# Cutting the last tile of a split-GELU kernel into steps of 1, 1, 2 and 4 rows

## Chip, cores, metric

One core of a Trainium2 chip. The metric is device time in microseconds (us), as a median of several executions; small is good. The profile's span is about 1.8 us shorter than the time of the same run, because it counts from the first to the last instruction.

## The reference

```python
x = randn(32, 512, 2048)                 # float32
x1, x2 = x[..., :1024], x[..., 1024:]
out = 0.5 * x1 * (1 + erf(x1 / sqrt(2))) * x2    # float32, (32, 512, 1024)
```

134 MB are read and 67 MB written, with one GELU and one product per output element.

## The kernel before

The 16,384 rows are cut into 16 tiles of 128 partitions x 8 rows. A tile is loaded by one transfer (8.39 MB) from SyncE's queue, two tiles ahead. ScalarE and VectorE work on it in two steps of four rows. The output of tiles 0 to 13 is stored by ScalarE's queue, 4.19 MB each; that of tile 14 by SyncE's queue; and the last tile has two stores of four rows (2.10 MB each) on SyncE's queue, each issued as soon as its four rows are done.

```python
    R, STEP = 8, 4
    ...
    xpool = ctx.enter_context(tc.tile_pool(name="xpool", bufs=2))
    opool = ctx.enter_context(tc.tile_pool(name="opool", bufs=2))
    ...
    for i in range(n_tiles):
        x_tile = ahead.pop(0)
        o_tile = opool.tile([P, R, half], out.dtype, name="o_tile")
        last = i == n_tiles - 1
        for r in range(0, R, STEP):
            rows = slice(r, r + STEP)
            nc.scalar.activation(                      # GELU, in place
                out=x_tile[:, rows, :half], in_=x_tile[:, rows, :half], func=GELU
            )
            nc.vector.tensor_mul(                      # product
                out=o_tile[:, rows, :], in0=x_tile[:, rows, :half], in1=x_tile[:, rows, half:],
            )
            if last:
                store(nc.sync, i, o_tile, rows)
        if not last:
            store(nc.sync if i == n_tiles - 2 else nc.scalar, i, o_tile, slice(0, R))
        if i + 2 < n_tiles:
            ahead.append(load(i + 2))
```

Of the kernel before, what the change touches and what calls it, by code (L numbers as in the profile page):

```python
# [1 line left out]

# [4 lines left out]

GELU = mybir.ActivationFunctionType.Gelu


@with_exitstack
def kernel(
    ctx: ExitStack,
    tc: tile.TileContext,
    x: bass.AP,
    out: bass.AP,
):





    nc = tc.nc
    P = nc.NUM_PARTITIONS

    x_flat = x.flatten_outer_dims()
    out_flat = out.flatten_outer_dims()
    n_rows, dim = x_flat.shape
    half = dim // 2

    R, STEP = 8, 4
    x_t = x_flat.rearrange("(n p r) d -> n p r d", p=P, r=R)
    o_t = out_flat.rearrange("(n p r) d -> n p r d", p=P, r=R)
    n_tiles = x_t.shape[0]

    xpool = ctx.enter_context(tc.tile_pool(name="xpool", bufs=2))
    opool = ctx.enter_context(tc.tile_pool(name="opool", bufs=2))

    def load(i):
        x_tile = xpool.tile([P, R, dim], x.dtype, name="x_tile")  # L40
        nc.sync.dma_start(out=x_tile, in_=x_t[i])  # L41
        return x_tile

    def store(queue, i, o_tile, rows):
        queue.dma_start(out=o_t[i][:, rows, :], in_=o_tile[:, rows, :])

    ahead = [load(0), load(1)]
    for i in range(n_tiles):
        x_tile = ahead.pop(0)
        o_tile = opool.tile([P, R, half], out.dtype, name="o_tile")  # L50
        last = i == n_tiles - 1
        for r in range(0, R, STEP):
            rows = slice(r, r + STEP)
            nc.scalar.activation(  # L54
                out=x_tile[:, rows, :half], in_=x_tile[:, rows, :half], func=GELU
            )
            nc.vector.tensor_mul(  # L57
                out=o_tile[:, rows, :],
                in0=x_tile[:, rows, :half],
                in1=x_tile[:, rows, half:],  # L60
            )
            if last:
                store(nc.sync, i, o_tile, rows)
        if not last:
            store(nc.sync if i == n_tiles - 2 else nc.scalar, i, o_tile, slice(0, R))
        if i + 2 < n_tiles:
            ahead.append(load(i + 2))


# [1 line left out]
_INS = ['x']  # L71
_OUTS = [((32, 512, 1024), 'float32')]


# [23 lines left out]
```

## Time and profile before

| | before |
|---|---|
| time, median of the first three runs | 471.6 us |
| span of the profiled run | 469.7 us |
| last load lands | 449.29 us |
| last product ends | 461.78 us |
| last store lands | 468.9 us |

Engine columns give the busy time, its share of the span and the number of instructions. The row of DMA digits is the busy share of the 16 DMA engines in 40 equal slices, in tenths. A timeline line has the start, the duration, the engine and line of the kernel, the operation, output and input, and in brackets how long the engine sat idle before it and what ended that. "SPq" and "ACTq" are the sequencers of SyncE and ScalarE, and such a line shows only the issue of a transfer; the transfer itself is told by its time "to landing". The prediction shows the lines of the kernel before.

One warning about the chain of waits of this kernel. It ends with the last tile's GELU and product, as if they set the end, because it follows instructions and no instruction but the closing wait stands behind the last store. That wait is in SyncE's own view of waits (waited for: us in total, times, longest us):

```profile
SPq L93 <- DMA out_dram<-o_tile: 6.6, 1, 6.6
```

### The profile page before, as it was taken

The page shows a single profiled execution, that of the slowest core. Times are in us where ns is not written, and L with a number is a line of the kernel's source. Part 1 is how long each engine was busy: PE and PEld are TensorE (multiplying, and loading weights), DVE is VectorE, ACT ScalarE, POOL GpSimd, SP SyncE. Part 2 cuts the span into 40 slices and gives each one's busy share as a digit, 9 for nine tenths or more (in the row PEclk, how much of TensorE's full clock was granted, in tenths as well). Part 3 has the DMA queues.
Part 4 walks back from the last instruction along what each step waited for, and adds up shares of the span by engine and source line. Part 5 has one row for each costly group of instructions (what it writes and reads, how often), then busy time and mean ns, then how long its engine had stood idle before and what let it go on. Part 6 is the DMA issues. An engine that isn't in the chain of part 4 may idle for free.

```text
span 469.7 us, 213 instructions
## 1 busy us (share of the span) xinstructions
DVE 140.2 (30%) x32; ACT 115.2 (25%) x33; POOL 0.2 (0%) x4
## 2 busy tenths in 40 slices
DVE  0070704307042070520606115060250702507043
ACT  1052306023060320603206041060500505005060
POOL 0000000000000000000000000000000000000000
DMA  8999999999999999999999999999999999999988
GB/s 357 446 446 357 446 446 446 402 446 458 391 446 444 433 463 402 435 413 491 402 419 430 491 402 402 446 491 402 402 446 480 413 402 444 449 446 402 474 375 357
DMA packets 4754, 201.35 MB, mean 429 GB/s; under 512 B 528, under 2 KB 528, under 8 KB 528
## 3 DMA queue, kind: packets, MB, share of 16 engines
q1 hardware_dynamic: 2736, 142.61, 70.5%
q10 hardware_dynamic: 2016, 58.72, 29.0%
q14 instruction: 2, 0.02, 0.0%
HBM read 134.22 MB, written 67.11 MB: 429 GB/s over the span
## 4 chain that ended last, share of the span: by engine, by line
DMA 77%; DVE 14%; ACT 6%; DVEq 1%; issue 0%; SPq 0%; ACTq 0%
DMA x_tile<-in_x_dram 77%; DVE o_tile L57 14%; ACT x_tile L54 6%; DVEq L93 1%; SPq L41 0%; ACTq L54 0%
## 5 line engine op out<-in xcount | busy, mean ns | idle before, releaser
L57 DVE TENSOR_TENSOR o_tile<-x_tile 128x4096 f32<-128x4096 f32 x32 | 140.2, 4422 | 321.6 <-ACT x_tile L54 321.6
L54 ACT ACTIVATE x_tile<-x_tile 128x4096 f32<-128x4096 f32 x32 | 114.0, 3608 | 340.5 <-DMA x_tile<-in_x_dram 340.5
L54 ACT ACT_TABLE_LOAD x1 | 1.3, 1283 | 0.7 <-PEq L82 0.7
L82 POOL MEMSET const-bfloat16-1.0<- 128x1 bf16 x1 | 0.1, 102 | 0.0
L82 POOL MEMSET const-uint8-127<- 128x1 uint8 x1 | 0.1, 101 | 0.0
L82 POOL MEMSET const-float32-0.0<- 128x1 f32 x1 | 0.1, 99 | 0.2 <-issue 0.2
L82 POOL MEMSET const-float32-1.0<- 128x1 f32 x1 | 0.1, 98 | 0.0
## 6 DMA issues: line engine op xcount, KB each, us to landing
out_dram<-o_tile ACTq DMA_DIRECT2D x14, 4096.0 KB, 41.8
out_dram<-o_tile SPq DMA_DIRECT2D x1, 4096.0 KB, 24.8
out_dram<-o_tile SPq DMA_DIRECT2D x2, 2048.0 KB, 6.9
x_tile<-in_x_dram SPq DMA_DIRECT2D x16, 45.5
```

Source lines behind the costliest of these rows:

```text
L54: nc.scalar.activation(out=x_tile[:, rows, :half], in_=x_tile[:, rows, :half], func=GELU)
L57: nc.vector.tensor_mul(out=o_tile[:, rows, :], in0=x_tile[:, rows, :half], in1=x_tile[:, rows, half:],)
L82: nc = _bacc.Bacc("TRN2", target_bir_lowering=False, num_devices=1)
L93: with _tile.TileContext(nc) as tc:
```

## The change

The intent: the first product of the last tile has to wait for a GELU of four rows, 3.6 us. With a first step of one row it waits for 1.05 us, so VectorE starts sooner, and both stores of the last tile can be issued sooner. The stores keep their size and their queue.

```diff
-    R, STEP = 8, 4
+    R = 8
@@
-        for r in range(0, R, STEP):
-            rows = slice(r, r + STEP)
+        for lo, hi in ((0, 1), (1, 2), (2, 4), (4, 8)) if last else ((0, 4), (4, 8)):
+            rows = slice(lo, hi)
@@
-            if last:
-                store(nc.sync, i, o_tile, rows)
+            if last and hi % 4 == 0:
+                store(nc.sync, i, o_tile, slice(hi - 4, hi))
```

## The prediction

> **What bounds the kernel now.** I read the page from the top: busy shares, the row of 40 slices, the DMA queues, then the chain that ended last. The whole kernel moves 201 MB and computes little.
>
> ```profile
> span 469.7 us, 213 instructions
> DVE 140.2 (30%) x32; ACT 115.2 (25%) x33; POOL 0.2 (0%) x4
> DMA  8999999999999999999999999999999999999988
> q1 hardware_dynamic: 2736, 142.61, 70.5%
> q10 hardware_dynamic: 2016, 58.72, 29.0%
> HBM read 134.22 MB, written 67.11 MB: 429 GB/s over the span
> ```
>
> VectorE and ScalarE are busy 30% and 25% of the time; the 16 DMA engines are at 8 or 9 tenths in every slice, and the two queues together take 99.5% of their time. So the transfers set the time, and computing faster can help only in a stretch in which the DMA engines would otherwise have nothing to do. The change touches only the last tile, so the question is whether there is such a stretch after the last load has landed.
>
> The queue sizes say who shares a queue. One load is 128 x 8 x 2048 x 4 bytes = 8.39 MB, one whole store is 4.19 MB, a half store 2.10 MB. 16 x 8.39 + 4.19 + 2 x 2.10 = 142.6 MB: this is q1, the queue of SyncE, with all loads and the last three stores. 14 x 4.19 = 58.7 MB is q10, ScalarE's queue, with the other 14 stores. Next the timeline of the end (start us, duration us, engine, line, operation):
>
> ```profile
> 405.29 0.36 ACTq L45 DMA_DIRECT2D out_dram<-o_tile  x1
> 434.51 27.63 SPq L45 DMA_DIRECT2D out_dram<-o_tile  x3
> 449.37 7.12 ACT L54 ACTIVATE x_tile<-x_tile 128x4096 f32<-128x4096 f32 x2 [20.18 <-DMA x_tile<-in_x_dram]
> 453.02 8.76 DVE L57 TENSOR_TENSOR o_tile<-x_tile 128x4096 f32<-128x4096 f32 x2 [18.54 <-ACT x_tile L54]
> ```
>
> The last load lands at 449.29 (the chain of waits has its DMA piece from 405.29 for 44.00 us) and ScalarE starts at 449.37. The last store from ScalarE's queue was issued at 405.29; a store there takes 41.8 us in the middle of the queue view's list, so it lands at about 447.1. After 449.3 the transfers are SyncE's three stores alone. Asked in narrow windows, the view of the output tensor gives each of these its issue and landing time:
>
> ```profile
> 434.51 0.35 SPq L45 DMA_DIRECT2D out_dram<-o_tile  x1
> DMA to landing us min/median/max: 24.8/24.8/24.8
> ...
> 457.48 0.34 SPq L45 DMA_DIRECT2D out_dram<-o_tile  x1
> DMA to landing us min/median/max: 6.6/6.6/6.6
> ...
> 461.81 0.33 SPq L45 DMA_DIRECT2D out_dram<-o_tile  x1
> DMA to landing us min/median/max: 7.1/7.1/7.1
> ```
>
> So the store of tile 14 lands at 434.51 + 24.8 = 459.3, the first half of the last tile at 457.48 + 6.6 = 464.1, the second half at 461.81 + 7.1 = 468.9; the program ends at 469.7, 0.8 us later. The steps between landings, from the last load on, are 10.0, 4.8 and 4.8 us for 4.19, 2.10 and 2.10 MB: 419, 437 and 437 GB/s. The middle of the kernel repeats two loads and two stores, 25.17 MB, every 57.9 us (the chain's DMA pieces start at 56.85, 114.92, 172.94): 434 GB/s. The two half stores thus follow each other at the full rate of the kernel. The store of tile 14, issued 15 us before the last load landed, stood behind that load in the same queue and fills the time in which the last tile is computed. Wider stretches agree:
>
> ```profile
> 449.29:459.31 10.02, 6.29 (x2) 7.12 (x2) 0.00 (x0) 1.00 0.97 418
> 459.31:468.40 9.09, 2.47 (x1) 0.00 (x0) 0.00 (x0) 1.00 0.96 406
> ```
>
> The last two columns are the DMA share and GB/s: 0.97 and 0.96 up to the end. Single microseconds swing between 0.5 and 1.5, because whole packets are put to one window, so a gap of a few tenths can't be excluded from the shares alone; the landing times are the better witness.
>
> **What the Trainium skill says.** "DMA: Bandwidth & Descriptors", section "Queues, rings and completion order": on each DMA engine the descriptors of one queue are consumed in ring order. The trace agrees: tile 14's store, 24.8 us under way, lands 10.0 us after the load ahead of it. Same page, "Where 436 GB/s comes from": the ports give 435.2 GB/s. The trace shows 434 in the steady part and 437 between the last landings (4.8 us rounded to a tenth), so there is no faster rate to be had in the tail. Same page, "Anatomy of one DMA": its fit, made on the GpSimd path, is 2.0 us plus bytes over 436 GB/s, which for 2.10 MB is 6.8 us. The trace has 6.6 and 7.1, which is close, and this feeds the main rival below. "VectorE: DVE Perf Modes", section "The TRN2 errata": ScalarE takes 224 cycles at 1.2 GHz besides one cycle per element, and an f32 tensor_tensor (N+151)/0.96 ns. For 4096 elements this is 3600 and 4424 ns; the trace has 3608 and 4422.
>
> **The change part by part.** Removed: one GELU and one product of 4096 elements per partition. Added: GELUs and products of 1024, 1024 and 2048. Both stores stay, with their bytes, queue and order. No other tile changes, so everything up to 449.37 stays.
>
> Estimated durations from those formulas, which the trace confirms for the one size it has: GELU 1.05 us for 1024, 1.90 for 2048, 3.61 for 4096 (as measured); product 1.22, 2.29, 4.42. Instructions on one engine overlap a little: the second GELU started at 452.90, 3.53 us after the first (0.08 less than its duration), and two products took 8.76, a step of 4.34 (also 0.08 less). I take 0.08 off each step, and 0.04 from a GELU's end to the product it releases.
>
> GELU ends: 450.42, 451.39, 453.21, 456.74; before, 456.49 (two more instructions at about 0.12 each). Products: the first 450.46 to 451.68; the second 451.60 to 452.82; the third waits for its GELU, 453.25 to 455.54; the fourth waits too, 456.78 to 461.20. Stores are issued about 0.04 after the product: the first half at 455.58 instead of 457.48, 1.90 us earlier; the second at 461.24 instead of 461.81, 0.57 us earlier. The second gains so little because ScalarE must still do all eight rows before the last product can start.
>
> Now the queue. Tile 14's store still lands at 459.3, since the load before it lands when it did. The first half is in the queue 3.7 us before that instead of 1.8, and lands at 459.3 + 4.8 = 464.1 as before. The second half is issued 2.9 us before that instead of 2.3, and lands at 468.9 as before. All 1.90 and all 0.57 us turn into longer time in the queue. Sum: 0.0 us on the path that sets the end, so 471.6 us, less a tenth for what the landings, rounded to a tenth, may hide: 471.5.
>
> **The rivals.** First: the end hangs on the issue of the second half, a fixed cost plus its wire time, rather than on the queue. For it: 7.1 us is near the 6.8 of the fit. Against it: the first half lands in 6.6 though tile 14's store still has 1.8 us to go at its issue, and 1.8 + 4.8 is exactly 6.6, as 2.3 + 4.8 is 7.1. If it is true, the end moves with the issue, at most 0.57 us: 471.0.
>
> Second: the queue ran dry for a moment before the first half, as start-up and tile 14's last bytes did not quite overlap; the weak microsecond 457 to 458, share 0.53, could be that. Against it: other microseconds are as weak (447 to 448 has 0.00, with a load in flight), and the step to the next landing is the plain wire time. The most it can give: 8.39 MB at 435.2 GB/s is 19.3 us, the trace has 19.6 from the last load's landing to the last store's. So at best 0.3 us: 471.3.
>
> Third: the steps cost more than estimated, or another wait appears. To lengthen the kernel, the second half's issue would have to come some 2 us later; two small GELUs with 0.12 us extra each are far from that. It would give 472 or a little more. I hold it for unlikely.
>
> **Range and chances.** The causes reach from 471.0 to 471.6. The three runs of the kernel before spread from 471.57 to 472.48, and a median of new runs can fall anywhere there or a few tenths below. So 471.5, with 470.8 to 472.2 for 8 in 10. A gain of 2% would be 9.4 us, more than the whole 7.9 us from the last product's end to the end of the span, and nothing in the change can save that; a loss of 2% would need a different state of the chip. Faster 0.01, same 0.98, slower 0.01.
>
> **What would show it.** In the changed kernel: four GELUs and four products after the last load, the first store issued near 455.6 and the second near 461.2 on the same clock. If I am right, their times to landing grow by the same amounts, to about 8.5 and 7.7 us, and the landings stay 4.8 us apart after tile 14's. If landing times stay at 6.6 or 7.1 and the span shrinks by half a microsecond, the first rival holds; if only the step to the first half's landing shrinks, the second. A change before 449 us, or a last product that ends later than 461.8, would make the working wrong.

## The result, and the profile after

The changed kernel takes 471.43 us (median of six runs, 471.36 to 471.85), the kernel before 471.54 us (six runs, 471.3 to 472.48). The ratio is 0.9997, with a 95% interval of 0.9984 to 1.001: no difference.

The page of the changed kernel:

```profile
span 470.1 us, 217 instructions
DVE 140.5 (30%) x34; ACT 115.4 (25%) x35; POOL 0.2 (0%) x4
DMA  8999999999999999999999999999999999999988
q1 hardware_dynamic: 2736, 142.61, 70.5%
```

The same queues with the same packets, the same DMA row, and two more instructions on each of the two engines. The profiled run was the slowest of the six (471.85 us, span 470.1); the other five have spans of 469.6 and 469.7. Its last load landed at 449.81, 0.52 us later than in the profile before, although nothing is changed up to there. So I count from the last load's landing in each profile.

The end of the timeline, and the two half stores of the last tile in the view of the output tensor, asked in narrow windows:

```profile
449.89 7.31 ACT L55 ACTIVATE x_tile<-x_tile 128x1024 f32<-128x1024 f32 x4 [20.42 <-DMA x_tile<-in_x_dram]
450.98 2.36 DVE L58 TENSOR_TENSOR o_tile<-x_tile 128x1024 f32<-128x1024 f32 x2 [16.23 <-ACT x_tile L55]
453.73 2.29 DVE L58 TENSOR_TENSOR o_tile<-x_tile 128x2048 f32<-128x2048 f32 x1 [0.39 <-ACT x_tile L55]
457.23 4.43 DVE L58 TENSOR_TENSOR o_tile<-x_tile 128x4096 f32<-128x4096 f32 x1 [1.21 <-ACT x_tile L55]
...
456.05 0.34 SPq L46 DMA_DIRECT2D out_dram<-o_tile  x1
DMA to landing us min/median/max: 8.4/8.4/8.4
...
461.69 0.33 SPq L46 DMA_DIRECT2D out_dram<-o_tile  x1
DMA to landing us min/median/max: 7.6/7.6/7.6
```

VectorE starts 1.17 us after the load instead of 3.73, but then waits twice for ScalarE (0.39 and 1.21 us), because ScalarE must do all eight rows in any case. From the last load's landing:

| us after the last load has landed | before | after |
|---|---|---|
| tile 14's store lands | 10.0 | 9.8 |
| first half issued / lands | 8.19 / 14.8 | 6.24 / 14.6 |
| second half issued / lands | 12.52 / 19.6 | 11.88 / 19.5 |

The issues come 1.95 and 0.64 us sooner; the times to landing grow from 6.6 to 8.4 and from 7.1 to 7.6; and the landings stay where they were, within the 0.2 us by which tile 14's store also differs. SyncE now waits that much longer at the end:

```profile
SPq L94 <- DMA out_dram<-o_tile: 7.1, 1, 7.1
```

It was 6.6. The time won on the engines has become waiting for the queue.

### The profile page after: what moved, and what is told of

Same layout as the page of the kernel before. It is cut to its first block, busy times and chain, and to the rows that moved or that the text cites. A ratio compares the mean times of both kernels' runs of the same rounds, so it can differ in the third digit from the quotient of the medians. Undisturbed runs are those within 1.5% of the kernel's fastest.

```text
span 470.1 us, 217 instructions
## 1 busy us (share of the span) xinstructions
DVE 140.5 (30%) x34; ACT 115.4 (25%) x35; POOL 0.2 (0%) x4
## 4 chain that ended last, share of the span: by engine, by line
DMA 77%; DVE 14%; ACT 7%; issue 0%; ACTq 0%; SPq 0%
DMA x_tile<-in_x_dram 77%; DVE o_tile L58 14%; ACT x_tile L55 7%; ACTq L94 0%; SPq L42 0%; ACTq L55 0%
## 5 line engine op out<-in xcount | busy, mean ns | idle before, releaser
L58 DVE TENSOR_TENSOR o_tile<-x_tile 128x4096 f32<-128x4096 f32 (+2 forms) x34 | 140.5, 4171 | 321.2 <-ACT x_tile L55 321.2
L55 ACT ACTIVATE x_tile<-x_tile 128x4096 f32<-128x4096 f32 (+2 forms) x34 | 114.2, 3407 | 341.0 <-DMA x_tile<-in_x_dram 341.0
```

Source lines behind the costliest of these rows:

```text
L55: nc.scalar.activation(out=x_tile[:, rows, :half], in_=x_tile[:, rows, :half], func=GELU)
L58: nc.vector.tensor_mul(out=o_tile[:, rows, :], in0=x_tile[:, rows, :half], in1=x_tile[:, rows, half:],)
```

## The experiments

**Theory**: the last three stores stand in one queue behind each other, and wire time sets the end. (Wire time is a transfer's bytes over the steady rate: 4.8 us for a half store, by the step between the last two landings.) **Rival**: the end hangs on when the second half is issued, and the 0.6 us that the issue gained was lost in noise or given back elsewhere. The runs were made in three calls, each on one chip. In the four runs of the first call the kernel before had a median of 471.57 us, in the next three 471.52, in the last two 471.57.

### The stores without the wait for the last tile

```diff
-                store(nc.sync, i, o_tile, slice(hi - 4, hi))
+                store(nc.sync, i, prev, slice(hi - 4, hi))     # prev: tile 14's output
@@
+        prev = o_tile
```

This gives a wrong result: the two half stores read the output tile of tile 14, so that they wait for nothing of the last tile, which is still computed.

> The changed kernel, but the two last stores read the output tile before it (wrong result on purpose), so they are issued right behind the store of tile 14, about 14 us before the last load lands; the last tile is still computed. Queue theory: the three stores land 19.3 to 19.6 us after the last load as before, the time moves by less than 0.3 us: nothing that computes the last tile sooner can gain more than this. Issue rival: with both issues 20 us earlier the span falls to where compute or wire ends, several us less.

Measured: 471.39 us (five runs, 471.34 to 471.79), ratio to before 0.9999 (0.9987 to 1.0012). The last load landed at 449.21. The store of tile 14 and the two half stores:

```profile
434.05 0.35 SPq L46 DMA_DIRECT2D out_dram<-o_tile  x1
DMA to landing us min/median/max: 25.1/25.1/25.1
...
434.44 0.47 SPq L46 DMA_DIRECT2D out_dram<-o_tile  x1
DMA to landing us min/median/max: 29.5/29.5/29.5
...
434.97 0.42 SPq L46 DMA_DIRECT2D out_dram<-o_tile  x1
DMA to landing us min/median/max: 33.9/33.9/33.9
```

The second half was in the queue 27 us sooner than in the changed kernel, and landed at 434.97 + 33.9 = 468.9, or 19.7 us after the load. That is no sooner than before (19.6). So nothing that computes the last tile faster can shorten this kernel, and the rival falls.

### Making the second half late

```diff
+            if last and hi == R:
+                for _ in range(k):                     # k = 1, 2, 6
+                    nc.vector.tensor_mul(out=o_tile[:, 7:8, :], in0=x_tile[:, 7:8, :half],
+                                         in1=x_tile[:, 7:8, half:])
             if last and hi % 4 == 0:
```

The last row's product is done again, which changes no value and costs about 1.25 us each time (some 1.1 had been expected).

> The changed kernel, with the product of the last row of the last tile done once more before the second half store: its issue comes about 1.14 us later, some 13.0 us after the last load has landed instead of 11.9; the result is unchanged. Queue theory (the stores stand in one queue and the wire sets the end): span and time move by 0 to 0.3 us, the second half's time to landing shrinks from 7.6 to about 6.5. Rival, the end hangs on the issue of the second half: time to landing stays 7.6 and the span grows by 1.1 us.

> The same with two repeated rows: issue about 2.2 us later, some 14.1 us after the last load. Queue theory with no start-up cost: still 0. Queue theory with a fixed cost of about 2 us that needs the store to be issued that long before its turn: the second half lands at about 14.1 + 6.8 = 20.9 us after the load instead of 19.5, the span grows by about 1.5 us. Issue rival: plus 2.2 us.

> The same with six repeated rows: issue about 6.8 us later, some 18.7 us after the last load, when the first half has long landed (14.6). This measures the time to landing of a half store in an empty queue: 4.8 us if it is wire time alone (span plus 4.0), 6.8 us with a fixed cost of 2 us (span plus 6.0). Issue rival: 7.6 us and span plus 6.8.

The second half store in the three profiles, k = 1, 2, 6 in this order:

```profile
462.17 0.33 SPq L46 DMA_DIRECT2D out_dram<-o_tile  x1
DMA to landing us min/median/max: 6.7/6.7/6.7
```

```profile
463.74 0.33 SPq L46 DMA_DIRECT2D out_dram<-o_tile  x1
DMA to landing us min/median/max: 6.3/6.3/6.3
```

```profile
468.68 0.33 SPq L46 DMA_DIRECT2D out_dram<-o_tile  x1
DMA to landing us min/median/max: 6.3/6.3/6.3
```

| k | last load lands | second half issued after it | to landing | time, median (range) | against before |
|---|---|---|---|---|---|
| 1 | 449.03 | 13.14 | 6.7 | 471.53 (471.41 to 471.74) | 1.0 (0.9987 to 1.0012) |
| 2 | 449.34 | 14.40 | 6.3 | 472.65 (472.63 to 472.82) | 1.0025 (1.0011 to 1.0039) |
| 6 | 449.24 | 19.44 | 6.3 | 477.73 (477.58 to 477.86) | 1.0131 (1.0117 to 1.0145) |

The issue is later than in the changed kernel by 1.26, 2.52 and 7.56 us; the time, against 471.43, is longer by 0.10, 1.22 and 6.30. The first delay of about 1.3 us is free, and beyond it each microsecond costs one: 2.52 - 1.3 = 1.22 and 7.56 - 1.3 = 6.26. (The 471.43 is from another call; counted from the kernel before of this call, 471.57, the free delay comes out as 1.4.) The time to landing shows why. With k = 6 the first half has landed at 455.5 + 8.4 = 463.9, 4.8 us before the issue, so the queue is empty and 6.3 us is the whole cost of a half store: 4.8 us on the wire and 1.5 us besides. The packets in this trace show where the 1.5 lies: none is under way for the first 0.83 us after the issue, they then run for 5.08 us, and the landing comes 0.35 us after the last of them. Any time to landing beyond 6.3 is waiting behind something. In the kernel before that was 0.3 us for the first half (6.6) and 0.8 us for the second (7.1); in the changed kernel it is 2.1 and 1.3 us. With k = 1 the store still waits 0.4 us, because in that profile the two stores ahead of it landed 0.4 us later after the load (10.2 and 15.0 us). Neither the full fixed cost of 2 us nor wire time alone, both named ahead of the k = 6 run, was right: it lies between them.

### The same delay in the kernel before

```diff
+            if last and r + STEP == R:
+                (the same repeated product, once)
             if last:
                 store(nc.sync, i, o_tile, rows)
```

> The kernel before (steps of 4 and 4), with the product of the last row repeated once, which makes its second half store about 1.25 us later. If a half store in an empty queue takes 6.3 us, as the delayed runs showed, the kernel before has 7.1 - 6.3 = 0.8 us to spare: time to landing falls to 6.3 and the time grows by about 0.45 us. If the spare time were the 2.3 us that the prediction counted, nothing would change. Issue rival: plus 1.25 us.

> The changed kernel once more, on the same chip as the run above: within 0.2 us of the kernel before; half stores with 8.4 and 7.6 us to landing; the last store lands 19.4 to 19.7 us after the last load, wherever that load lands.

Measured: 471.92 us (five runs, 471.89 to 472.11) with the delay, and 471.41 us (471.29 to 471.92) for the changed kernel run again on the same chip. The ratio of the delayed kernel to the kernel before is 1.0004 (0.9991 to 1.0016). That alone is inconclusive, because some runs of the kernel before were themselves slow this time (up to 472.75). The trace of the delayed kernel before is plainer:

```profile
463.00 0.33 SPq L45 DMA_DIRECT2D out_dram<-o_tile  x1
DMA to landing us min/median/max: 6.3/6.3/6.3
```

The load landed at 449.22, the second half at 469.3, 20.1 us later instead of 19.6. The store waits for nothing ahead of it, as with k = 2 and 6, and lands some 5.4 us behind the first half (457.41 + 6.4 = 463.8) instead of 4.8. One and the same delay of 1.25 us thus cost the kernel before 0.35 us by the medians and some 0.5 by the landings, which agrees with 1.25 - 0.8 = 0.45, and cost the changed kernel nothing that the runs resolve. What the change bought is spare time, and nothing used it.

The repeat of the changed kernel confirmed its time but missed one of the numbers expected: 8.8 and 8.0 us to landing instead of 8.4 and 7.6, and the last store landed 19.9 us after the load (461.37 + 8.0 - 449.50). Tile 14's store in that profile landed 10.2 us after the load and not 9.8; the queue ahead was 0.4 us later and both halves with it. So single profiles differ by that much, and the 0.1 us between before and after in the last column of the table above means nothing.

### A tail without the store in front

```diff
-            store(nc.sync if i == n_tiles - 2 else nc.scalar, i, o_tile, slice(0, R))
+            store(nc.scalar, i, o_tile, slice(0, R))
```

Tile 14's store is put on ScalarE's queue, so it no longer stands between the last load and the half stores in SyncE's queue. It was tried with steps of 4 and 4 and with the changed steps.

> The kernel before, with the store of tile 14 issued from ScalarE's queue instead of SyncE's, so that it no longer stands behind the last load but runs beside it. Queue theory: the last load lands some 2 us later (about 451.6), tile 14's store near 459, the first half store is issued at about the same time into a queue that is just empty, and the span grows by 2 to 3 us over the kernel before. Issue rival: the end follows the load by the same 19.6 us, also plus 2 us.

> The changed kernel with the store of tile 14 on ScalarE's queue. Queue theory: with less ahead in the queue the earlier issues count, and it is about 0.6 to 1.1 us faster than the partner with steps of 4 and 4 in this call. Issue rival: 0.6 us faster, as it should have been in the kernel as changed.

Measured: 472.74 us (five runs, 472.56 to 473.54) with steps of 4 and 4, and 472.09 (471.95 to 472.33) with the changed steps: 0.65 us apart, and no run of one within the range of the other. The first half stores, of 4 and 4 and of the changed steps:

```profile
459.02 0.35 SPq L45 DMA_DIRECT2D out_dram<-o_tile  x1
DMA to landing us min/median/max: 6.3/6.3/6.3
```

```profile
457.29 0.35 SPq L46 DMA_DIRECT2D out_dram<-o_tile  x1
DMA to landing us min/median/max: 7.6/7.6/7.6
```

With 4 and 4 the load lands at 450.84, and the first half is issued 8.18 us later, as tile 14's store lands (434.62 + 24.7 = 459.3). 6.3 us to landing says that its full fixed cost lies open. With the changed steps the load lands at 451.05 and the issue comes 6.24 us later, 1.94 sooner; 7.6 - 6.3 = 1.3 us of this is waiting, and the other 0.6 us are won. Here the change does what it was meant to do, and it is still worth 0.14%. Both versions are slower than both kernels. With a store beside it the last load lands 1.2 to 1.6 us later than in the same steps before, so the half stores are issued later too. Tile 14's store still lands at 459.3 and 459.5, where it did; what is lost is lost behind it, since the first half lands about 6 and 5.4 us after it and not 4.8. With 4 and 4 this comes to 1.2 us over the kernel before of the same call (471.52); 2 to 3 us had been expected, which was too much.

### One step of eight rows

```diff
-        for lo, hi in ((0, 1), (1, 2), (2, 4), (4, 8)) if last else ((0, 4), (4, 8)):
+        for lo, hi in ((0, 8),) if last else ((0, 4), (4, 8)):
@@
+            if last:                                   # both half stores after the one product
+                store(nc.sync, i, o_tile, slice(0, 4))
+                store(nc.sync, i, o_tile, slice(4, 8))
```

> The kernel before with the last tile in one step of 8 rows (one GELU, one product), then the same two half stores. The product ends about 15.7 us after the last load (7.0 + 8.7), so both stores are issued there, 6 us after tile 14's store has landed. Queue theory: the queue is dry, they land at about 15.7 + 2.0 + 9.6 = 27.3 us after the load, the span grows by 7 to 8 us (1.6%). Rival, the second half's issue plus about 7 us: plus 3.3 us.

Measured: 479.01 us (five runs, 478.78 to 479.7), ratio 1.0161 (1.0147 to 1.0175).

```profile
449.78 7.03 ACT L55 ACTIVATE x_tile<-x_tile 128x8192 f32<-128x8192 f32 x1 [20.34 <-DMA x_tile<-in_x_dram]
456.85 8.69 DVE L58 TENSOR_TENSOR o_tile<-x_tile 128x8192 f32<-128x8192 f32 x1 [22.11 <-ACT x_tile L55]
...
465.56 0.34 SPq L46 DMA_DIRECT2D out_dram<-o_tile  x1
DMA to landing us min/median/max: 6.3/6.3/6.3
...
465.96 0.42 SPq L46 DMA_DIRECT2D out_dram<-o_tile  x1
DMA to landing us min/median/max: 10.8/10.8/10.8
```

Here the queue is empty for 6.1 us, from tile 14's store (434.76 + 24.7 = 459.5) to the issue. The first half takes 6.3 us again, and the second lands 4.9 us behind it, about its wire time. So steps matter as long as they leave the queue dry: from one step to two, 7.5 us are won; from two to four, nothing.

No experiment points to a version that beats both kernels. The run whose half stores wait for nothing of the last tile shows that this tail has no more to give on the compute side.

## Why the prediction was right

**What sets the end**: right. The prediction had the stores of the tail queued at the full rate of the wire, and the run with unhindered half stores, which landed its last store after the same 19.6 to 19.7 us, shows it. The time alone could not have: the first two rivals came to 471.0 and 471.3, so near that all of them would have looked like no change. The landings tell them apart. (One reading was off without consequence: the starts quoted for the steady part are 58.0 us apart, not 57.9; the 434 GB/s stands.)

**The new durations**: right. The groups by shape have these means (busy us, mean ns of one):

```profile
L58 DVE TENSOR_TENSOR o_tile<-x_tile 128x1024 f32<-128x1024 f32 x2 | 2.4, 1222 | 16.2 <-ACT x_tile L55 16.2
L58 DVE TENSOR_TENSOR o_tile<-x_tile 128x2048 f32<-128x2048 f32 x1 | 2.3, 2293 | 0.4 <-ACT x_tile L55 0.4
L55 ACT ACTIVATE x_tile<-x_tile 128x1024 f32<-128x1024 f32 x2 | 2.0, 1049 | 20.4 <-DMA x_tile<-in_x_dram 20.4
L55 ACT ACTIVATE x_tile<-x_tile 128x2048 f32<-128x2048 f32 x1 | 1.9, 1895 | 0.0
```

1.22, 2.29, 1.05 and 1.90 us had been estimated. The issues were put at 6.29 and 11.95 us after the load and came at 6.24 and 11.88; the times to landing were to be 8.5 and 7.7 and were 8.4 and 7.6.

**The spare time in the queue**: too large. The working counted the store's whole stay behind the one ahead, 1.8 and 2.3 us in the kernel before, as wire time of the other store still to go ("1.8 + 4.8 is exactly 6.6"). The sum was right, but its parts were not: a half store needs 6.3 us and not 4.8 even alone, so the kernel before had only 0.3 and 0.8 us to spare. The statement that the second half would have to come some 2 us later to lengthen the kernel is therefore off: measured 1.3 us for the changed kernel, about 0.8 for the kernel before.

**The first rival** had a true core, the fixed cost, but not its consequence: as long as the store is issued early enough, the fixed cost passes while the store ahead is on the wire. **The second rival**, a moment with the queue dry before the first half, was true in part. A count of the packets under way in the trace of the kernel before shows fewer than 16 from 458.0 to 458.4, down to 4 at 458.3; as a mean over the 16 engines that is 0.2 us of idle time. In the changed kernel, and in the run with unhindered half stores, the count stays at 16 there. But the landing was not held up by it: the first half still landed 4.8 us behind tile 14's store. If anything was won it is the 0.1 us between the medians (471.52 to 471.57 against 471.43 and 471.41), which the intervals do not resolve. Where the margin was gone, with tile 14's store on the other queue, 0.65 us were won.

## What to carry to other kernels

At the end of a transfer-bound kernel, take the landing times of the last few transfers and not the end of the last instruction: if they are spaced by bytes over the steady rate, as here, finishing the compute sooner only lengthens the wait in the queue. To learn how much spare time there is, subtract the time to landing of a like transfer in an empty queue from the one observed, or delay the issue on purpose until the time moves. Before building a finer cut of a tail, a kernel whose stores wait for nothing tells in one run what the best cut could be worth. Its output is wrong, which doesn't matter for the time.

## What the Trainium skill lacked or had wrong

- "DMA: Bandwidth & Descriptors", section "Anatomy of one DMA": its fit of 2.0 us plus bytes over 436 GB/s is for transfers issued on the GpSimd path, and that section gives none for SyncE's. Here a 2.10 MB store from SyncE's queue, with nothing in flight ahead of it (k = 6 and the single step of eight rows), took 6.3 us; the fit gives 6.8. The cost besides the wire's 4.8 us was 1.5 us.
- The same page, "Queues, rings and completion order", tells the order of a queue, but neither it nor another section says how much of this fixed cost passes behind the transfer ahead. Here a half store issued 1.8 us or more before the landing of the store ahead landed 4.8 to 4.9 us behind it, that is at wire time alone; issued 0.8 us before (the delayed kernel before) it landed some 5.4 us behind, and 0.2 us before (k = 2) some 6.1.
- "VectorE: DVE Perf Modes", section "The TRN2 errata": nothing was wrong here; estimates from its formulas held within 1% at the new sizes (products of 1222 and 2293 ns against 1224 and 2291, GELUs of 1049 and 1895 ns against 1040 and 1893).
